# Splitting the last contraction's tokens into 384 and 128 instead of two halves of 256, with the second part's output products on VectorE alone

## The chip, the cores and the metric

The kernel runs on one core of a Trainium2 chip. The metric is the device time of one execution in microseconds, as the median of several runs. TensorE (PE) multiplies matrices into PSUM, VectorE (DVE), ScalarE (ACT) and GpSimd (POOL) work on elements, and SyncE (SP) issues the transfers between memory and the core's buffers.

## The reference, cut to what matters

Two layers on an input of 512 tokens with 1024 channels, all in float32. The whole ends like this:

```
h = h + (silu(gate) * val) @ w_down        # w_down: 2816 x 1024, layer 1
y = h * rsqrt(mean(h*h over channels) + 1e-6) * final_norm_g
```

Only these two lines bear on the change: the last down-projection's contribution to the residual h, and the final norm, whose mean runs over all 1024 channels of a token, so that no token's output can be formed before the last channel tile of that token is done.

## The kernel before

The residual h lies in SBUF with channels on the partitions: eight tiles (d = 0 to 7) of 128 channels by 512 tokens, together `hall`. A float32 product is made of three matmuls in rounded fp32 (fp32r): `mms` (lines 145 to 151) multiplies, for every block of 128 input channels, the weights' high part with the data's high part, the high with the low, and the low with the high. Each of these matmuls loads its own 128 x 128 weights.

The down-projection of layer 1 has 22 input blocks. They are done in chunks; the last chunk, blocks 18 to 21, is done by `last_down` (lines 842 to 863) in two parts of H = 256 tokens, so that the final norm of the first part can run beside the contraction of the second. A part t consists of eight channel tiles; `half` makes one tile with 4 x 3 = 12 matmuls, and `final_tile` (lines 867 to 881) then adds the result to h on VectorE (through the helper at line 418), squares it on ScalarE (line 876), sums the squares into `acc` on GpSimd (line 880; those of the last two tiles go to the statistics as separate inputs), and scales h by the norm's weight on ScalarE (line 881). The weights of all eight tiles are kept, and the eight tiles of part 1 follow those of part 0 in the order of the program.

`stats` (line 184) sums the squares over the channels with small fp32 matmuls (`sum_mm`, line 213: for each block of 128 tokens two matmuls of 64 columns, for each of three inputs). Every plain fp32 matmul shows as two instructions in the trace. `inv_rms_sqrt` (lines 216 to 226) makes the reciprocal root with a ScalarE square root, a VectorE reciprocal and a Newton step. `spreader` (line 236) then spreads it over the 128 partitions with one fp32 matmul per block of 128 tokens (line 241) into the PSUM tile `pbc`, and copies that to SBUF on ScalarE (`rs`, line 244), because GpSimd takes its factor from SBUF. `pst` and `pbc` share one PSUM buffer. `final_out` (lines 883 to 891) multiplies: four products of two tiles each (512 elements per partition), three on VectorE with `pbc` as factor, the fourth on GpSimd with `rs`; each product is stored by a transfer from SyncE's queue.

The program's order around the end is: the eight tiles of part 0; tile 0 of part 1; the statistics of part 0; tiles 1 to 3; the output of part 0; tiles 4 to 7; statistics and output of part 1. The framework's scheduler may shift single instructions within this.

Of the kernel before, what the change touches and what calls it, by code (L numbers as in the profile page):

```python
# [9 lines left out]
F32 = mybir.dt.float32  # L10
# [3 lines left out]
ALU = mybir.AluOpType  # L14
PSUM = bass.MemoryType.PSUM

P = 128
T = 512
KD = 8
NFF = 22  # L20
CH = (((0, 8), (8, 16), (16, 22)), ((0, 6), (6, 12), (12, 18)))
H = T // 2
EPS = 1e-6
LAG = (2, 3)
LATE = 2
# [28 lines left out]
def trunk(ctx: ExitStack, tc: tile.TileContext, x, pra, prb, eva, evu, evv, evo, evos, bmat, bmatz, cmat, wglu,  # L54
          wst, bs, odi, odo, up, dn, out):
    nc = tc.nc
    V, G, S, PE = nc.vector, nc.gpsimd, nc.scalar, nc.tensor

    cp = ctx.enter_context(tc.tile_pool(name="cp", bufs=1))
# [6 lines left out]
    def pt(name):  # L66
        return ps.tile([P, T], F32, tag="mm", name=name)

    def gt(name, dt=F32R):
        return gp.tile([P, T], dt, tag="g", name=name)  # L70
# [3 lines left out]
    hall = cp.tile([P, KD, T], F32, name="hall")  # L74
# [8 lines left out]
    warm = gt("warm", F32)  # L83
    V.memset(warm[:, :H], 1.0)
    pwarm = ps2.tile([P, T], F32, tag="aux", name="pwarm")
    for _ in range(NWARM):
        PE.matmul(pwarm[:, :H], lhsT=warm[:, :P], rhs=warm[:, :H], start=True, stop=True)
    onesd = cp.tile([P, 2], F32, name="onesd")
    V.memset(onesd, 1.0 / (KD * P))
    epsb = cp.tile([P, 1], F32, name="epsb")  # L90
    epsq = cp.tile([P, 1], F32, name="epsq")
    V.memset(epsb, EPS)
    S.activation(epsq, epsb, AF.Square)
# [51 lines left out]
    def mms(dst, hi, lo, xs, ks, first, last):  # L145
        for k in ks:
            xh, xl = xs[k]
            c = slice((k - first) * P, (k - first + 1) * P)
            PE.matmul(dst, lhsT=hi[:, c], rhs=xh, start=(k == first), stop=False)  # L149
            PE.matmul(dst, lhsT=hi[:, c], rhs=xl, start=False, stop=False)  # L150
            PE.matmul(dst, lhsT=lo[:, c], rhs=xh, start=False, stop=(k == last))  # L151
# [21 lines left out]
    def newton(m, y, n, tag):  # L173
        t = cp.tile([P, 8], F32, tag="nt", name=f"nt{tag}", bufs=2)[:, :n]
        ti = t.bitcast(I32)
        yi = y.bitcast(I32)
        V.tensor_scalar(out=ti, in0=m.bitcast(I32), scalar1=1, scalar2=None, op0=ALU.arith_shift_right)
        V.tensor_scalar(out=yi, in0=ti, scalar1=-1, scalar2=0x5F3759DF, op0=ALU.mult, op1=ALU.add)
        for _ in range(3):
            V.scalar_tensor_tensor(out=t, in0=y, scalar=-0.5, in1=y, op0=ALU.mult, op1=ALU.mult)  # L180
            V.tensor_tensor(out=t, in0=t, in1=m, op=ALU.mult)
            V.scalar_tensor_tensor(out=y, in0=t, scalar=1.5, in1=y, op0=ALU.add, op1=ALU.mult)

    def stats(tag, t0=0, n=4, extra=(), inv=None):


        parts = [acc[:, t0 * P:(t0 + n) * P]] + list(extra)
        pst = ps2.tile([P, T], F32, tag="aux", name=f"pst{tag}")
        for q, a in enumerate(parts):
            sum_mm(pst, a, n, q == 0, q == len(parts) - 1)  # L190
        return (inv or inv_rms)(pst, tag, n)

    def wide_stats(tag):
# [5 lines left out]
        def spread():  # L199
# [4 lines left out]
            V.scalar_tensor_tensor(out=t, in0=y, scalar=-0.5, in1=y, op0=ALU.mult, op1=ALU.mult)  # L204
            V.scalar_tensor_tensor(out=t, in0=pst, scalar=EPS, in1=t, op0=ALU.add, op1=ALU.mult)
            V.scalar_tensor_tensor(out=y, in0=t, scalar=1.5, in1=y, op0=ALU.add, op1=ALU.mult)
# [3 lines left out]
    def sum_mm(pst, a, n, first, last):  # L210
        for i in range(n):
            for e in (0, 64):
                PE.matmul(pst[e:e + 64, 2 * i:2 * i + 2], lhsT=a[:, i * P + e:i * P + e + 64], rhs=onesd,
                          start=first and i == 0, stop=last and i == n - 1)

    def inv_rms_sqrt(pst, tag, n):
# [3 lines left out]
        S.activation(s, src, AF.Sqrt, bias=epsb)  # L220
        V.tensor_scalar(out=m, in0=src, scalar1=EPS, scalar2=None, op0=ALU.add)
        V.reciprocal(y, s)
# [5 lines left out]
    def inv_rms(pst, tag, n):  # L228
        m = cp.tile([P, 8], F32, tag="m", name=f"m{tag}", bufs=2)[:, :n]
        y = cp.tile([P, 8], F32, tag="rt", name=f"rt{tag}", bufs=2)[:, :n]  # L230
        V.tensor_scalar(out=m, in0=pst[:, :2 * n].rearrange("p (i t) -> p i t", t=2)[:, :, 0],
                        scalar1=EPS, scalar2=None, op0=ALU.add)
        newton(m, y, n, tag)
        return y, spreader(y, tag, n)

    def spreader(y, tag, n):
        def spread():
            w = min(n, 4)
            pbc = ps2.tile([P, T], F32, tag="aux", name=f"pbc{tag}")
            for i in range(w):  # L240
                PE.matmul(pbc[:, i * P:(i + 1) * P], lhsT=y[:, i:i + 1].to_broadcast([P, P]), rhs=ident,
                          start=True, stop=True)
            rs = cp.tile([P, T], F32, tag="rs", name=f"rs{tag}")
            S.copy(rs[:, :w * P], pbc[:, :w * P])
            return rs, pbc
        return spread
# [29 lines left out]
    fsq = {}  # L276
# [78 lines left out]
    def v_norm():  # L355
        ss = sp.tile([P, 4], F32, name="ss")
        rv = sp.tile([P, 4], F32, name="rv")
        for t in range(4):
            q = sp.tile([P, 768], F32, tag="vsq", name=f"vsq{t}")
            S.activation(q, vg[t], AF.Square, accum_out=ss[:, t:t + 1])  # L360
        V.tensor_scalar(out=ss, in0=ss, scalar1=1.0 / 768.0, scalar2=EPS, op0=ALU.mult, op1=ALU.add)
        newton(ss, rv, 4, "v")
# [54 lines left out]
    def ttt(o, a, b, op):  # L417
        V.tensor_tensor(out=o, in0=a, in1=b, op=op)  # L418
# [422 lines left out]

    def last_down(gk, a, d):
        def half(t, e, hi, lo):
            p = pt(f"pl{t}_{e}")[:, :H]
            c = slice(t * H, (t + 1) * H)
            mms(p, hi, lo, {k: (gk[k][0][:, c], gk[k][1][:, c]) for k in range(a, NFF)},
                range(a, NFF), a, NFF - 1)
            final_tile(t, e, p)

        def f(hi, lo):  # L850
            kept.append((hi, lo))
            half(0, d, hi, lo)
            if d == 0:
                S.activation(epsq, acc[:, :1], AF.Sqrt)
            if d == KD - 1:
                for e in range(KD):
                    half(1, e, *kept[e])
                    if e == 0:
                        y0 = stats("fin0", 0, 2, fsq[0], inv_rms_sqrt)
                    if e == 3:  # L860
                        final_out(0, y0)
                final_out(1, stats("fin1", 2, 2, fsq[1], inv_rms_sqrt))
        return f

    kept = []

    def final_tile(t, d, p):
        c = slice(t * H, (t + 1) * H)
        ttt(h[d][:, c], h[d][:, c], p, ALU.add)
        if d == 0:  # L870
            S.activation(acc[:, c], h[d][:, c], AF.Square)
        else:
            late = d >= KD - 2
            sq = (gt(f"sqf{t}_{d}", F32) if late else
                  cp.tile([P, T], F32, tag="sq", name=f"sqf{t}_{d}", bufs=2))[:, :H]
            S.activation(sq, h[d][:, c], AF.Square)
            if late:
                fsq.setdefault(t, []).append(sq)
            else:
                G.tensor_tensor(out=acc[:, c], in0=acc[:, c], in1=sq, op=ALU.add)  # L880
        S.activation(h[d][:, c], h[d][:, c], AF.Copy, scale=pb[:, B_GFIN + d:B_GFIN + d + 1])

    def final_out(t, y):
        rs, pbc = y[1]()
        c = slice(t * H, (t + 1) * H)
        for q in range(4):
            o = gt(f"out{t}_{q}", F32).rearrange("p (d t) -> p d t", t=H)
            e, r = (G, rs) if q == 3 else (V, pbc)
            e.tensor_tensor(out=o, in0=hall[:, 2 * q:2 * q + 2, c],
                            in1=r[:, :H].unsqueeze(1).to_broadcast([P, 2, H]), op=ALU.mult)  # L890
            nc.sync.dma_start(out[t, :, 2 * q:2 * q + 2, :], o)

    def next_norm(col, tag, new):
        def f(d):
# [118 lines left out]
    w = gt("onesw", F32)[:, :P]  # L1013
# [87 lines left out]
```

## Time and profile before

| | us |
|---|---|
| median of 3 runs | 1064.66 |
| lowest and highest | 1063.97, 1065.13 |
| the profiled execution | 1063.25 |
| its span, first to last instruction | 1061.5 |
| mean granted TensorE clock | 0.998 of full speed |

The profile comes from one execution, whose own time is 1.4 us under the median. Times in the trace's rows are microseconds from the start of the span; a row of the timeline gives start, duration, engine, line, operation, output and inputs, shapes and the count of instructions merged into it. Matmuls are pipelined: the recorded duration of one is longer than the distance to the next one's start, so that a price of a matmul in a stream is read from starts.

### The profile page before, as it was taken

Reading aid. Unit: us, or ns where it says so; the run is one execution under the profiler, and the core shown is the slowest. Engines: PE = TensorE matmul, PEld = TensorE weight load, DVE = VectorE, ACT = ScalarE, POOL = GpSimd, SP = SyncE. Lnnn points to the kernel's source line nnn. Section 1 sums busy time; section 2 is a strip of 40 time slices with the busy share of each in tenths; the row PEclk is TensorE's granted clock in tenths of the full one; section 3 lists DMA queues with packets and bytes.
Section 4 is the critical chain, followed back from the end, with each engine's and each line's share of the span. In section 5 each row is a group of like instructions: output and inputs, shape, how many; then the busy total and the mean of one; then the engine's idle time right before and its main releaser. Section 6 shows DMA issues by size and latency. Waiting matters only on the chain.

```text
span 1061.5 us, 12932 instructions
## 1 busy us (share of the span) xinstructions
PE 1049.3 (99%) x5098; PEld 875.9 (83%) x5098; DVE 669.5 (63%) x926; ACT 421.3 (40%) x567; POOL 134.4 (13%) x120
## 2 busy tenths in 40 slices
PE   9999999999999999999999999999999999999997
PEld 7978788888888888888888888888888888888886
DVE  7996679866356653566576564678645664666543
ACT  5563355443133431344423222444423432444344
POOL 3010031110001000012211110302100100011002
PEclk9999999999999999999999999999999999999999
DMA  7362332333332332223322321423233223222222
GB/s 261 123 130 81 99 100 99 101 98 99 100 99 99 96 90 96 97 80 89 130 93 86 99 99 60 139 84 102 73 120 99 90 81 128 98 93 79 88 80 80
DMA packets 40125, 107.21 MB, mean 101 GB/s; under 512 B 10368, under 2 KB 11392, under 8 KB 40064
## 3 DMA queue, kind: packets, MB, share of 16 engines
q1 hardware_dynamic: 39920, 106.12, 32.0%
q8 instruction: 40, 0.66, 0.3%
q10 hardware_dynamic: 144, 0.26, 0.1%
q14 instruction: 21, 0.17, 0.0%
HBM read 103.08 MB, written 3.28 MB: 100 GB/s over the span
## 4 chain that ended last, share of the span: by engine, by line
PE 97%; ACT 1%; DMA 1%; DVE 0%; SPq 0%; issue 0%; POOL 0%; DVEq 0%; ACTq 0%; POOLq 0%
PE pf L151 15%; PE pf L150 15%; PE pf L149 15%; PE pd L151 11%; PE pd L150 11%; PE pd L149 11%; PE po L151 1%; PE po L149 1%; PE po L150 1%; PE pe L149 1%; PE pe L150 1%; PE pe L151 1%; PE pv L314 1%; PE pv L315 1%; PE pv L313 1%; PE phu L149 1%
## 5 line engine op out<-in xcount | busy, mean ns | idle before, releaser
L125 ACT CAST whi<-raw 128x1024 fp32r<-128x1024 f32 (+2 forms) x203 | 198.4, 980 | 450.5 <-PE pd L150 200.7
L151 PE MATMUL pf<-xhf,wlo 128*128 128x512 f32 x704 | 273.9, 389 | 0.0
L150 PE MATMUL pf<-xlf,whi 128*128 128x512 f32 x704 | 273.6, 389 | 0.0
L149 PE MATMUL pf<-xhf,whi 128*128 128x512 f32 x704 | 273.5, 389 | 0.0
L126 DVE TENSOR_TENSOR wlo<-raw,whi 128x1024 fp32r<-128x1024 f32 (+3 forms) x204 | 246.5, 1209 | 39.9 <-ACT whi L125 39.6
L150 PEld LDWEIGHTS pf<-xlf,whi 128*128 128x128 f32 x704 | 132.2, 188 | 27.8 <-DVE xlf L159 0.2
L149 PEld LDWEIGHTS pf<-xhf,whi 128*128 128x128 f32 x704 | 132.2, 188 | 27.5
L151 PEld LDWEIGHTS pf<-xhf,wlo 128*128 128x128 f32 x704 | 132.2, 188 | 27.2
L418 DVE TENSOR_TENSOR hs<-pf,rsf 128x512 f32<-128x512 f32 x88 | 60.5, 691 | 126.4 <-PE pf L151 126.3
L815 POOL TENSOR_TENSOR cv<-cv,cv 128x512 f32<-128x512 f32 x44 | 58.5, 1329 | 571.6 <-DVE cv L788 529.3
L418 DVE TENSOR_TENSOR hall<-hall,pd 128x512 f32<-128x512 f32 x48 | 32.9, 686 | 101.1 <-PE pd L151 101.1
L151 PE MATMUL pd<-xhm,wlo 128*128 128x512 f32 x192 | 74.7, 389 | 0.0
L150 PE MATMUL pd<-xlm,whi 128*128 128x512 f32 x192 | 74.7, 389 | 0.0
L149 PE MATMUL pd<-xhm,whi 128*128 128x512 f32 x192 | 74.7, 389 | 0.0
L786 ACT ACTIVATE cv<-hs,pb 128x512 f32<-128x512 f32 x88 | 71.3, 815 | 7.4 <-DVE hs L418 6.0
L788 DVE SCALAR_TENSOR_TENSOR cv<-hs,pb,cv 128x512 f32<-128x512 f32 x88 | 66.1, 751 | 2.7
L787 DVE SCALAR_TENSOR_TENSOR cv<-hs,pb,cv 128x512 f32<-128x512 f32 x88 | 67.5, 769 | 0.0
L812 ACT ACTIVATE cv<-cv 128x512 f32<-128x512 f32 x44 | 27.8, 632 | 81.5 <-DVE cv L788 81.4
L149 PEld LDWEIGHTS pd<-xhm,whi 128*128 128x128 f32 x192 | 36.0, 188 | 7.6
L150 PEld LDWEIGHTS pd<-xlm,whi 128*128 128x128 f32 x192 | 36.0, 188 | 7.5
L151 PEld LDWEIGHTS pd<-xhm,wlo 128*128 128x128 f32 x192 | 36.0, 188 | 7.4
L171 POOL TENSOR_TENSOR acc<-acc,sqf 128x512 f32<-128x512 f32 x14 | 23.1, 1653 | 56.4 <-ACT sqf L170 56.1
(587 smaller groups left out, 1569.7 us busy)
## 6 DMA issues: line engine op xcount, KB each, us to landing
raw<-up SPq DMA_DIRECT2D x88, 512.0 KB, 3.4
raw<-dn SPq DMA_DIRECT2D x32, 384.0 KB, 3.2
raw<-odi SPq DMA_DIRECT2D x24, 512.0 KB, 3.4
raw<-dn SPq DMA_DIRECT2D x16, 512.0 KB, 3.5
raw<-odo SPq DMA_DIRECT2D x8, 512.0 KB, 3.4
raw<-evo SPq DMA_DIRECT2D x8, 384.0 KB, 3.2
raw<-eva SPq DMA_DIRECT2D x7, 384.0 KB, 6.6
raw<-evu SPq DMA_DIRECT2D x5, 512.0 KB, 4.5
```

The lines of the kernel that those rows point to most:

```text
L125: S.copy(hi[:, c], r[:, c])
L126: V.tensor_tensor(out=lo[:, c], in0=r[:, c], in1=hi[:, c].bitcast(F32), op=ALU.subtract)
L149: PE.matmul(dst, lhsT=hi[:, c], rhs=xh, start=(k == first), stop=False)
L150: PE.matmul(dst, lhsT=hi[:, c], rhs=xl, start=False, stop=False)
L151: PE.matmul(dst, lhsT=lo[:, c], rhs=xh, start=False, stop=(k == last))
L171: eng.tensor_tensor(out=acc, in0=acc, in1=sq, op=ALU.add)
L418: V.tensor_tensor(out=o, in0=a, in1=b, op=op)
L786: S.activation(o, src[:, 2:T + 2], AF.Identity, scale=w2, bias=b)
L787: V.scalar_tensor_tensor(out=o, in0=src[:, 1:T + 1], scalar=w1, in1=o, op0=ALU.mult, op1=ALU.add)
L788: V.scalar_tensor_tensor(out=o, in0=src[:, 0:T], scalar=w0, in1=o, op0=ALU.mult, op1=ALU.add)
L812: S.activation(c, c, AF.Silu)
L815: G.tensor_tensor(out=c, in0=c, in1=fp["gate"], op=ALU.mult)
```

## The change

The token parts become 0 to 384 and 384 to 512 (`TP`). The statistics of the first part cover three blocks of 128 tokens, those of the second one block. The output of part 0 is made in eight products of one tile (384 elements), of which GpSimd takes three and VectorE five; the output of part 1 in four products of two tiles (256 elements), all on VectorE from PSUM, and the copy of the factor to SBUF is left out there. The output tensor is laid out accordingly, and the host puts the parts together.

```
+TP = ((0, 384), (384, 512))
...
     def spreader(y, tag, n):
-        def spread():
+        def spread(copy=True):
...
+            if not copy:
+                return None, pbc
             rs = cp.tile([P, T], F32, tag="rs", name=f"rs{tag}")
             S.copy(rs[:, :w * P], pbc[:, :w * P])
             return rs, pbc
...
         def half(t, e, hi, lo):
-            p = pt(f"pl{t}_{e}")[:, :H]
-            c = slice(t * H, (t + 1) * H)
+            c = slice(*TP[t])
+            p = pt(f"pl{t}_{e}")[:, :c.stop - c.start]
...
-                        y0 = stats("fin0", 0, 2, fsq[0], inv_rms_sqrt)
+                        y0 = stats("fin0", 0, 3, fsq[0], inv_rms_sqrt)
                     if e == 3:
                         final_out(0, y0)
-                final_out(1, stats("fin1", 2, 2, fsq[1], inv_rms_sqrt))
+                final_out(1, stats("fin1", 3, 1, fsq[1], inv_rms_sqrt))
...
     def final_tile(t, d, p):
-        c = slice(t * H, (t + 1) * H)
+        c = slice(*TP[t])
...
     def final_out(t, y):
-        rs, pbc = y[1]()
-        c = slice(t * H, (t + 1) * H)
-        for q in range(4):
-            o = gt(f"out{t}_{q}", F32).rearrange("p (d t) -> p d t", t=H)
-            e, r = (G, rs) if q == 3 else (V, pbc)
-            e.tensor_tensor(out=o, in0=hall[:, 2 * q:2 * q + 2, c],
-                            in1=r[:, :H].unsqueeze(1).to_broadcast([P, 2, H]), op=ALU.mult)
-            nc.sync.dma_start(out[t, :, 2 * q:2 * q + 2, :], o)
+        rs, pbc = y[1](copy=t == 0)
+        c = slice(*TP[t])
+        w = c.stop - c.start
+        n = t + 1
+        for q in range(KD // n):
+            dd = slice(n * q, n * q + n)
+            o = gt(f"out{t}_{q}", F32)[:, :n * w].rearrange("p (d t) -> p d t", t=w)
+            e, r = (G, rs) if t == 0 and q in (2, 5, 7) else (V, pbc)
+            e.tensor_tensor(out=o, in0=hall[:, dd, c],
+                            in1=r[:, :w].unsqueeze(1).to_broadcast([P, n, w]), op=ALU.mult)
+            a = KD * c.start + n * w * q
+            nc.sync.dma_start(out[:, a:a + n * w].rearrange("p (d t) -> p d t", t=w), o)
```

## Rows read from the trace of the kernel before

**Rows 1.** The page: TensorE's busy time, share of the span and instructions (with the other engines'), the granted clock in 40 slices of the span, and the engines' shares of the chain that ended last.

```profile
PE 1049.3 (99%) x5098; PEld 875.9 (83%) x5098; DVE 669.5 (63%) x926; ACT 421.3 (40%) x567; POOL 134.4 (13%) x120
...
PEclk9999999999999999999999999999999999999999
...
PE 97%; ACT 1%; DMA 1%; DVE 0%; SPq 0%; issue 0%; POOL 0%; DVEq 0%; ACTq 0%; POOLq 0%
```

**Rows 2.** The chain of waits at the end, in order of time: start and length in us, engine, output, line.

```profile
1051.83 0.13 PE pl L151
...
1051.99 0.43 DVE hall L418
...
1052.44 0.42 ACT sqf L876
...
1052.89 0.51 ACT hall L881
1053.40 0.23 ACT srfin L220
...
1054.62 0.70 PE pbcfin L241 x4
...
1055.39 0.38 ACT rsfin L244
...
1055.80 0.69 DVE out L889
```

**Rows 3.** Timeline of TensorE: first and last start of 9 matmul distances at 384 columns (the first projection), and of 24 at 256 columns (the second part of the last contraction).

```profile
41.51 0.33 PE L313 MATMUL pv<-whi,xhm 128*128 128x384 f32 x1
...
43.07 0.33 PE L313 MATMUL pv<-whi,xhm 128*128 128x384 f32 x1
...
1047.47 0.28 PE L149 MATMUL pl<-g_18h,whi 128*128 128x256 f32 x1
...
1050.35 0.28 PE L149 MATMUL pl<-g_18h,whi 128*128 128x256 f32 x1
```

**Rows 4.** Groups by line and form, weight loads (PEld): count, busy us, mean ns of one, idle before.

```profile
L149 PEld LDWEIGHTS pl<-g_18h,whi 128*128 128x128 f32 x16 | 3.1, 191 | 0.1
...
L213 PEld LDWEIGHTS pstfin<-onesd,sqf 128*64 128x64 f32 x32 | 1.3, 137 | 0.6 <-ACT sqf L876 0.5
```

**Rows 5.** Timeline: two weight loads that follow the gating step's short matmuls, and 18 of those matmuls (plain fp32, 128 columns, two instructions for each product).

```profile
84.61 0.19 PEld L149 LDWEIGHTS phu<-xhm,whi 128*128 128x128 f32 x1
84.73 0.19 PEld L150 LDWEIGHTS phu<-xlm,whi 128*128 128x128 f32 x1
...
104.31 2.27 PE L396 MATMUL pg<-wt,vg 128*128 128x128 f32 x18
```

**Rows 6.** Timeline of TensorE: statistics matmuls of part 0 (8 for one input), the spread of part 0, and the spread of part 1. One recorded matmul lasts 0.20 us in the first kind and 0.275 in the others.

```profile
1040.11 0.40 PE L213 MATMUL pstfin<-onesd,acc 128*64 128x2 f32 x8
...
1045.96 0.60 PE L241 MATMUL pbcfin<-ident,rtfin 128*128 128x128 f32 x4
...
1054.62 0.68 PE L241 MATMUL pbcfin<-ident,rtfin 128*128 128x128 f32 x4 [1.31 <-DVE rtfin L225]
```

**Rows 7.** Groups by line and form of VectorE, ScalarE and GpSimd: count, busy us, mean ns of one, idle before. The adds at 256 and 512 columns, squares at 256 and 512, scales at 256 and 512, GpSimd's sums at 256 and products at 512.

```profile
L418 DVE TENSOR_TENSOR hall<-hall,pl 128x256 f32<-128x256 f32 x16 | 6.6, 420 | 13.0 <-PE pl L151 13.0
L418 DVE TENSOR_TENSOR hall<-hall,pd 128x512 f32<-128x512 f32 x48 | 32.9, 686 | 101.1 <-PE pd L151 101.1
...
L876 ACT ACTIVATE sqf<-hall 128x256 f32<-128x256 f32 x14 | 5.7, 415 | 6.8 <-DVE hall L418 5.4 <-DVE ntfin L224 1.3
L170 ACT ACTIVATE sqf<-hall 128x512 f32<-128x512 f32 x14 | 8.6, 618 | 0.0
L881 ACT ACTIVATE hall<-hall,pb 128x256 f32<-128x256 f32 x16 | 8.0, 507 | 0.4
L158 ACT ACTIVATE xhf<-hall,pb 128x512 fp32r<-128x512 f32 x16 | 11.5, 720 | 5.2 <-DVE hall L418 5.2
...
L880 POOL TENSOR_TENSOR acc<-acc,sqf 128x256 f32<-128x256 f32 x10 | 7.4, 739 | 43.5 <-ACT sqf L876 43.5
L889 POOL TENSOR_TENSOR out<-hall,rsfin 128x512 f32<-128x512 f32 x2 | 2.6, 1286 | 4.4 <-ACT rsfin L244 4.4
```

**Rows 8.** Timeline of VectorE: the three products of part 0, and the two adds that had waited behind them.

```profile
1047.03 1.88 DVE L889 TENSOR_TENSOR out<-hall,pbcfin 128x512 f32<-128x512 f32 x3 [0.81 <-ACT rsfin L244]
1048.83 0.74 DVE L418 TENSOR_TENSOR hall<-hall,pl 128x256 f32<-128x256 f32 x2
```

**Rows 9.** Timeline of SyncE's queue: the issues of part 1's output. The third and fourth are merged in one row, which ends 0.91 us after the third's start; a row of the fourth alone stands below it.

```profile
1056.51 0.33 SPq L891 DMA_DIRECT2D out<-out  x1
...
1057.11 0.33 SPq L891 DMA_DIRECT2D out<-out  x1
...
1057.54 0.91 SPq L891 DMA_DIRECT2D out<-out  x2
...
1058.04 0.41 SPq L891 DMA_DIRECT2D out<-out  x1
```

**Rows 10.** The transfers of part 1's output, GB/s in 40 slices of 0.15 us from 1056 to 1062 us; and the time from issue to landing of the eight output transfers.

```profile
GB/s 0 0 0 0 0 0 0 0 41 314 382 396 410 342 382 396 410 341 383 396 410 341 383 396 396 341 410 123 0 0 0 0 0 0 0 0 0 0 0 0
...
DMA to landing us min/median/max: 2.1/2.3/3.1
```

**Rows 11.** The waits between 1050 and 1062 us: who waited for whom, us in total, times, longest.

```profile
DVE out L889 <- ACT rsfin L244: 1.3, 1, 1.3
```

More of the change, by code (lines that the diff above doesn't have):

```diff
@@ L874, in final_tile @@
             sq = (gt(f"sqf{t}_{d}", F32) if late else
-                  cp.tile([P, T], F32, tag="sq", name=f"sqf{t}_{d}", bufs=2))[:, :H]
+                  cp.tile([P, T], F32, tag="sq", name=f"sqf{t}_{d}", bufs=2))[:, :c.stop - c.start]
             S.activation(sq, h[d][:, c], AF.Square)
@@ L1094 @@
             for n in _INS]
-    args.append(nc.dram_tensor("out", (2, P, KD, T // 2), F32, kind="ExternalOutput").ap())
+    args.append(nc.dram_tensor("out", (P, KD * T), F32, kind="ExternalOutput").ap())
     with _tile.TileContext(nc, schedule_with_timeline_sim=True) as tc:
@@ L1099 @@
     got = r.results[0]["out"]
-    return _np.ascontiguousarray(got.transpose(0, 3, 2, 1)).reshape(1, T, KD * P)
+    parts = [got[:, KD * a:KD * b].reshape(P, KD, b - a).transpose(2, 1, 0) for a, b in TP]
+    return _np.ascontiguousarray(_np.concatenate(parts, axis=0)).reshape(1, T, KD * P)
```

## Prediction

> **What bounds the kernel now.** I read the page first: TensorE is busy 99% of the span, 97% of the chain that ended last is TensorE, and the granted clock is full (2.4 GHz, a digit 9) in all forty slices [rows 1]. So a microsecond added to TensorE's stream is a microsecond of the kernel. Then the end of the chain of waits [rows 2]: after the last contraction matmul (1051.83 + 0.13 = 1051.96) TensorE only serves a serial tail: add, square, scale, square root, small VectorE steps, spread matmuls, a ScalarE copy, products, transfers, until 1061.5. That is 9.54 us during which the kernel is bound by latencies. The change trades between these two stretches: it adds to the stream and cuts the tail. The other views give prices: starts of matmuls by width [rows 3], weight loads [rows 4, 5], the statistics matmuls [rows 6], durations by shape [rows 7], VectorE and SyncE in order [rows 8, 9], the transfers [rows 10] and the waits [rows 11].
>
> **The change, part by part.** The sum is made against the profiled execution, 1063.25 us; the median of the runs is 1064.66, so I add the difference to the median. About 2.1 us (0.2%) is what a measurement of this kernel can tell from no change.
>
> *First part, 384 columns.* 8 tiles x 12 matmuls = 96. At 256 columns, 24 matmuls lie between two starts 2.88 us apart: 0.1200 us each; at 384 columns, 9 take 1.56 us: 0.1733 [rows 3]. 96 x 0.0533 = **+5.1 us**, all on TensorE.
>
> *Second part, 128 columns.* Again 96 matmuls, each with its own 128-column weight load. The trace has no rounded-fp32 (fp32r) matmul of 128 columns, so I bound it. The line through the two widths falls 0.000417 us per column and leaves 0.0133 at zero columns; at 128 columns it gives 0.067 us: lower end. Above, the nearest row of that width is the plain fp32 matmul of the gating step: two instructions for each product, 18 instructions in 2.27 us, less one's 0.275 of depth over 17 steps = 0.117 each [rows 5], so 0.235 a product; without the small loss per instruction the two take 2 x 0.108 (the spread matmuls: (0.60 - 0.275)/3 [rows 6]) = 0.216: upper end. Between them the weight load decides. A load of 64 columns is recorded with 137 ns and one of 128 with 191 [rows 4]: 54 ns for 64 columns, so 0.108 us of a 128-column load is throughput and only the rest is pipeline depth. With the 0.0133 that every fp32r matmul here pays, that is **0.121 us**, whatever the stream is. The two loads at 84.61 and 84.73, behind the gating step's short matmuls, stand 0.12 apart [rows 5], and that is the row nearest to the case: a load that waits for nothing but the load before it. Then the second part costs 96 x (0.121 - 0.120) = **+0.1 us**: the shorter matmuls save nothing. By 0.067 the term would be -5.1 us, by 0.216 it would be +9.2.
>
> A rule that gives another price: the Trainium skill, "TensorE: Matmul & The Clock Gate", section "Back-to-back issue gap", has about 81 ns for each matmul in a stream of load and matmul pairs of 128 columns. With it, as an estimate, the term would be -3.7 us and the whole change about -0.7 us; no run here has shown such a stream in fp32r, and the lengths of the loads [rows 4] speak against it.
>
> *Statistics of the first part.* Three column blocks instead of two: each of three inputs takes 12 matmul instructions instead of 8, so 12 more at (0.40 - 0.20)/7 = 0.029 us [rows 6] = +0.35 us; its spread takes 6 instead of 4 at 0.108 [rows 6] = +0.22. Together **+0.6 us** on TensorE.
>
> *First output.* Eight products of one tile (384 elements) instead of four of 512, five on VectorE, three on GpSimd, and eight transfers instead of four. Not on the end's path as long as the second part lasts: from its fourth tile to its end are 4 x 12 x 0.121 = 5.8 us. VectorE needs five products of about 0.55 us (between 0.42 for 256 and 0.69 for 512 [rows 7]), some 2.5 us, and its adds wait meanwhile, as they did before (three products, 1.88 us, then two adds together [rows 8]). GpSimd does three at about 1.0 us (between its 0.74 for 256 and 1.29 for 512 [rows 7]), ahead of the sums of squares of tiles 4 and 5; all of that ends over a microsecond before the last tile. SyncE issues eight at about 0.43 us [rows 9], 3.4 us, with nothing queued behind but the last output. If that cover is gone (second part short), it costs up to 1.7 us; see the first rival. In the first part a tile takes 2.08 us of TensorE, more than its add (0.55), its square and scale (0.52 + 0.61) or its GpSimd sum (1.0): hidden.
>
> *Tail.* Per step, from [rows 2, 7]: the add 0.42 to 0.29 (slope (0.686 - 0.420)/256 per column): -0.13. The square 0.415 to 0.31: -0.10. The scale, which stands ahead of the square root on ScalarE, 0.51 to 0.40: -0.11. The square root and the four small VectorE steps: unchanged, they are all overhead. The spread, two instructions instead of four: (0.68 - 0.275)/3 = 0.135 each [rows 6]: -0.27. The copy: VectorE's products wait today for ScalarE's copy of the same PSUM tile [rows 11], 1055.32 to 1055.80; without it they follow TensorE directly: -0.46. The products: three of 512 on VectorE last 1.88 us [rows 8]; four of 256 take 0.42 + 3 x 0.32 (two adds of that size took 0.74 [rows 8]) = 1.38: -0.50. GpSimd's product (1.29) ran beside them and isn't missed. So the last product ends 1.57 us sooner. Transfers: before, 1.05 MB kept the DMA engines full from about 1057.2 to 1060.2 [rows 10], 2.16 us beyond the last issue at 1058.04 [rows 9]. Now 0.52 MB comes in pieces of 128 KB that need about 0.36 us each at the same rate, less than the 0.43 between issues, so nothing piles up: 0.75 us from issue to data plus 0.36 = 1.1 us beyond the last issue: -1.05. If a transfer instead needs its shortest recorded 2.1 us to land [rows 10], nothing is gained there. Tail: **-2.6 us**, bounds -1.6 and -2.8.
>
> *Sum.* 5.1 + 0.1 + 0.6 - 2.6 = **+3.2 us**: 1066.4 in the profiled execution, 1067.8 against the median, 0.3% slower. With 0.108 to 0.130 for the short matmul (-1.2 to +0.9) and the tail's bounds: +1.7 to +5.1.
>
> **Rivals.**
> *The short matmul streams at its width (not slower).* If a 128-column load hides behind 0.067 us, the two parts cost TensorE what two of 256 did: 96 x (0.1733 + 0.0667 - 0.2400) = 0, and 0.6 - 2.6 = -2.0 us remain: 1062.7. But then tiles come every 0.80 us, and after the fourth only 3.2 us are left: VectorE's five products and four adds need about 3.6 us, and ScalarE's squares and scales (0.71 a tile) can only follow; up to 1.7 us of the gain goes into that, so 1062.7 to 1064.4. For: the line through two widths is straight to 256. Against: the load rows. It decides from a price of 0.109 on: below that the change is no longer slower by more than 0.2%. The Trainium skill's "TensorE: Matmul & The Clock Gate", section "Wait — 56ns, not 53.3ns?", has the width over 2.4 GHz plus about 2.5 ns between matmuls back to back, which is this rival's rule; the rows here agree in the slope and show 13 ns, not 2.5, beside it [rows 3].
> *A short fp32r matmul falls back to the price of plain fp32.* 96 x (0.216 - 0.121) = +9.1 more: +12.3, 1077.0. For: 256 is the narrowest fp32r operand anywhere in this trace, so nothing shows that the single pass holds below. Against: from 384 to 256 columns the price falls with the width, with no sign of a step to come.
> *The copy's removal removes no wait* (the products then wait as long for something else): 0.46 of the gain is gone, 1068.3; inside the forecast's range.
>
> **How the numbers follow.** Load-bound at about 0.12: 0.60. Streaming: 0.22. Plain fp32's price: 0.15. Anything else, a scheduler that orders the end otherwise for instance: 0.03. The prediction is the first case, 1067.8; its own range is 1066.4 to 1069.8. The range given reaches down to the streaming case, 1062.7, and up to 1070.0; it leaves out the plain-fp32 case and small tails. Slower by over 0.2% (above 1066.8): 0.60 x 0.78 + 0.15 + 0.01 = 0.63. Faster (below 1062.5): 0.22 x 0.4 + 0.01 = 0.10. Within: 0.27.
>
> **What the profile after would show.** Starts 0.173 apart in the first part; in the second 0.12 apart if I am right, 0.067 or 0.22 if a rival is, with the weight loads at the same distance. The last contraction matmul some 5.8 us later than before; from it to the end of the span some 6.9 us instead of 9.5; the products starting within 0.05 us of the spread's end with no ScalarE copy between; four issues about 0.43 apart and no backlog of transfers. I am wrong if short matmuls start much under 0.11 apart, or if the tail stays above 8 us.

## The result, and the profile after

The changed kernel took 1067.31 us (median of 19 runs), the kernel before, in runs beside it, 1064.14 (19 runs): 3.2 us or 0.3% slower. The ratio of all the runs is 1.0050, with a 95% interval of 1.0033 to 1.0066. It is larger than that of the medians because the runs of the changed kernel are spread in a way that those of before are not: twelve lie between 1065.4 and 1067.8, seven between 1072.6 and 1077.6. The kernel before stays between 1062.6 and 1066.3. The profiled execution is one of the seven: 1072.95 us, span 1071.2.

First the page of the changed kernel: TensorE's row, and the granted clock in 40 slices.

```profile
span 1071.2 us, 12944 instructions
...
PE 1060.6 (99%) x5098; PEld 887.4 (83%) x5098; DVE 669.7 (63%) x929; ACT 421.2 (39%) x566; POOL 135.4 (13%) x121
...
PEclk9999999999999999999999999999999999999995
```

TensorE's busy time has grown by 11.3 us with the same number of matmuls [rows 1], and the last slice of the clock shows a 5. The view by stretches says where: the wide part, the narrow part in two pieces, and the rest. After the stretch come its length, busy us (and instructions) of PE, PEld, DVE, ACT, POOL, then the granted clock, DMA share and GB/s.

```profile
1026.70:1043.40 16.70, 16.70 (x98) 16.70 (x97) 4.56 (x8) 9.37 (x16) 5.07 (x5) 1.00 0.00 1
1043.40:1048.70 5.30, 5.30 (x72) 5.12 (x71) 1.77 (x8) 2.57 (x7) 0.21 (x1) 1.00 0.00 0
1048.70:1063.20 14.50, 14.50 (x71) 14.38 (x70) 3.76 (x10) 3.87 (x12) 4.98 (x8) 0.50 0.31 110
1063.20:1071.20 8.00, 1.72 (x15) 1.29 (x14) 2.40 (x10) 0.97 (x3) 0.00 (x0) 0.50 0.20 66
```

From about 1048.7 us on TensorE runs at 1.2 GHz instead of 2.4, in the middle of the second part's narrow matmuls and without having been idle: it is busy for 5.30 of the 5.30 us ahead of the fall. The timeline of TensorE shows the matmuls on both sides of it:

```profile
1048.19 0.27 PE L150 MATMUL pl<-g_20h,whi 128*128 128x128 f32 x1
1048.30 0.28 PE L151 MATMUL pl<-g_20l,whi 128*128 128x128 f32 x1
1048.41 0.28 PE L152 MATMUL pl<-g_20h,wlo 128*128 128x128 f32 x1
1048.52 0.28 PE L150 MATMUL pl<-g_21h,whi 128*128 128x128 f32 x1
...
1048.97 0.41 PE L150 MATMUL pl<-g_18h,whi 128*128 128x128 f32 x1
1049.18 0.41 PE L151 MATMUL pl<-g_18l,whi 128*128 128x128 f32 x1
1049.39 0.41 PE L152 MATMUL pl<-g_18h,wlo 128*128 128x128 f32 x1
1049.61 0.41 PE L150 MATMUL pl<-g_19h,whi 128*128 128x128 f32 x1
```

Three narrow matmuls take 0.33 us before the fall and 0.64 after it: 0.111 and 0.213 each, against 0.120 for the 256-column ones of before [rows 3]. Some sixty of them at the lower clock cost 60 x 0.102 = 6.1 us; the spread's six matmuls (1.59 us instead of 0.88 in e8 below) and the tail (7.96 instead of 7.49) make up most of the rest of the 7.5 us by which this execution lies above the fastest ones (1065.4). With all 96 at half clock it would be 9.8 us plus the same rest, an estimate that comes to the runs at 1077; none of these was profiled.

The same kernel profiled a second time (e8 below) did not fall until the end. Its stretches, in the same columns, are those that answer to the prediction's sum:

```profile
1028.50:1045.30 16.80, 16.80 (x99) 16.76 (x98) 4.57 (x8) 9.37 (x16) 5.07 (x5) 1.00 0.00 1
1045.30:1058.30 13.00, 13.00 (x141) 12.75 (x141) 5.44 (x18) 6.31 (x18) 5.21 (x8) 1.00 0.19 65
1058.30:1061.10 2.80, 1.07 (x14) 0.73 (x14) 1.00 (x7) 0.92 (x3) 0.00 (x0) 1.00 0.75 267
```

The first of its wide and the first of its narrow matmuls, 96 wide ones apart (16.67 us, 0.1736 each):

```profile
1028.59 0.33 PE L150 MATMUL pl<-g_18h,whi 128*128 128x384 f32 x1
...
1045.26 0.22 PE L150 MATMUL pl<-g_18h,whi 128*128 128x128 f32 x1
```

And the end of its chain of waits, which answers to [rows 2]:

```profile
1058.18 0.13 PE pl L152
...
1058.33 0.30 DVE hall L421
...
1058.65 0.32 ACT sqf L879
...
1059.00 0.40 ACT hall L884
1059.40 0.22 ACT srfin L221
...
1060.29 0.17 DVE rtfin L226
...
1060.60 0.47 PE pbcfin L242 x2
...
1061.09 0.42 DVE out L895
```

In that execution the last contraction lasts from its first matmul at 1028.59 to 1058.31, 29.72 us; before it was 1027.07 to 1051.96, 24.89. That is +4.83. From there to the end of the span (1065.8) are 7.49 us instead of 9.54: -2.05. Together +2.8 us, with a full clock. The kernels here also differ from execution to execution by steps of some 2 us, because the clock is at half for a moment around 65 us in some (granted 1.00, 0.89 or 0.77 between 55 and 70 us). That fall is of another kind: TensorE had been idle ahead of it (in e8 it was busy for 0.10 of the 1.00 us from 64 to 65). Hence spans are compared from the first matmul of the last contraction, and medians over all runs.

### The profile page after: what moved, and what is told of

It reads as the page before. It is cut to its first block, busy times and chain, and to the rows that moved or that the text cites. A ratio compares the mean times of both kernels' runs of the same rounds, so it can differ in the third digit from the quotient of the medians.

```text
span 1071.2 us, 12944 instructions
## 1 busy us (share of the span) xinstructions
PE 1060.6 (99%) x5098; PEld 887.4 (83%) x5098; DVE 669.7 (63%) x929; ACT 421.2 (39%) x566; POOL 135.4 (13%) x121
## 4 chain that ended last, share of the span: by engine, by line
PE 98%; ACT 1%; DMA 0%; DVE 0%; issue 0%; SPq 0%; POOL 0%; DVEq 0%; POOLq 0%
PE pf L151 15%; PE pf L150 15%; PE pf L152 15%; PE pd L150 11%; PE pd L151 11%; PE pd L152 11%; PE po L152 1%; PE po L150 1%; PE po L151 1%; PE pe L150 1%; PE pl L150 1%; PE pl L152 1%; PE pl L151 1%; PE pv L317 1%; PE pe L151 1%; PE pe L152 1%
```

## The experiments

Each run's number of executions and range is given with its median; "before" beside them had medians of 1064.5 to 1064.7 throughout (27 to 29 runs in each batch).

**e1_equal_nocopy**: the tail's part of the change alone, on the kernel before.

```
-        rs, pbc = y[1]()
+        rs, pbc = y[1](copy=t == 0)
...
-            e, r = (G, rs) if q == 3 else (V, pbc)
+            e, r = (G, rs) if t == 0 and q == 3 else (V, pbc)
```

> The kernel before (two parts of 256) with one part of the change alone: in the second part's output the factor isn't copied to SBUF and all four products (512 elements) are on VectorE from PSUM. Theory 1 (the products waited for the copy): they start 0.46 us sooner behind the spread, four of them last 2.5 us instead of 1.9, the transfers start 0.46 sooner and stay the bound: 0.5 us faster than before, within a measurement's error. Theory 2 (another wait takes the copy's place): no change to 0.2 us slower. Under both, every contraction matmul starts 0.120 us after the one before, and the clock is full in all runs up to the last contraction matmul.

Measured: 1063.97 us (12 runs, 1062.32 to 1065.88), ratio to before 0.9993 (0.9983 to 1.0003); a second time, as **e11_equal_nocopy_again**, 1063.89 (11 runs, 1062.31 to 1065.58), 0.9996 (0.9986 to 1.0007).

> e1_equal_nocopy again, beside e9 and e10: 0.4 to 0.6 us faster than the kernel before in like runs, as in its first measurement, 1064.0.

The chain of waits of e1 has the first product directly behind the spread:

```profile
1055.96 0.70 PE pbcfin L241 x4
...
1056.68 0.69 DVE out L891
```

0.02 us instead of 0.48 [rows 2]: the wait for the copy is gone and none took its place. From the last contraction matmul (1053.30) to the end (1062.4) it is 9.1 us instead of 9.54, so 0.44 of the expected 0.46 arrives. Theory 1 holds in the profile; in the times the gain is 0.6 us of medians twice, which the intervals don't separate from nothing.

**e2_split_only**: the split with the copy and GpSimd's product back.

```
-        rs, pbc = y[1](copy=t == 0)
+        rs, pbc = y[1]()
...
-            e, r = (G, rs) if t == 0 and q in (2, 5, 7) else (V, pbc)
+            e, r = (G, rs) if q in ((2, 5, 7) if t == 0 else (3,)) else (V, pbc)
```

> The changed kernel with the split into 384 and 128 alone: in the second part's output the copy is back, and the fourth product is on GpSimd as before. Expected: the contraction as in the changed kernel, 0.173 us a matmul in the first part, 0.111 or 0.213 in the second, with the clock falling at a moment that differs from run to run; the tail 0.3 to 0.5 us longer than the changed kernel's. If the clock's fall belonged to the part without the copy, this one would show none: the runs would then all lie within 2 us of each other.

Measured: 1067.86 us (10 runs), seven between 1065.7 and 1067.9, three between 1076.7 and 1077.7; ratio 1.0057 (1.0029 to 1.0086). So the runs about 10 us above the others, which are the falls, come with the split and not with the missing copy. Its profiled execution had none until 1058 us; from the last contraction matmul (1056.10) to the end (1064.0) are 7.9 us, 0.4 more than in the changed kernel, as expected.

**e3_wide256** and **e4_wide192**: the second part's matmuls take 256, or 192, columns, of which the last 128 are used.

```
-            p = pt(f"pl{t}_{e}")[:, :c.stop - c.start]
+            w = 256 if t else c.stop - c.start
+            c = slice(c.stop - w, c.stop)
+            p = pt(f"pl{t}_{e}")[:, :w]
...
-            final_tile(t, e, p)
+            final_tile(t, e, p[:, w - (TP[t][1] - TP[t][0]):])
```

> The changed kernel, but the second part's 96 matmuls take 256 columns (tokens 256 to 511) and only the last 128 of the result are used: twice the columns for the same weight loads, everything else alike. Theory 1 (the clock falls because the second part's matmuls are narrow: TensorE streams only 128 columns for each 128-column load): starts 0.120 apart, full clock in every run up to the last contraction matmul, and 96 x 0.009 = 0.9 us over the changed kernel's undisturbed runs (1065.4): 1066.3, all runs within 1.5 us of each other, none above 1070. Theory 2 (it falls because of the waits at the statistics and the output, or of where the part stands): runs up to 1078 as in the changed kernel.

> As e3_wide256 with 192 columns. Theory 1 (a 128-column weight load sets the distance of short matmuls): starts 0.111 us apart at full clock, the same as at 128 columns. Theory 2 (the distance follows the columns below some width too): 0.0133 + 192 x 0.000417 = 0.093. For the clock: if narrowness decides, falls are rarer or later than at 128 columns; with none of them the time is 1065.4 by theory 1 and 1063.7 by theory 2.

Measured: e3 1068.59 us (5 runs, 1068.34 to 1069.33), ratio 1.0036 (1.0023 to 1.0050); e4 1067.10 (12 runs, 1065.32 to 1069.17), ratio 1.0023 (1.0013 to 1.0033). No run of either lies above 1070. The second part of e3, and that of e4, by stretches:

```profile
1045.40:1059.30 13.90, 13.90 (x141) 13.47 (x139) 5.53 (x18) 6.40 (x18) 5.25 (x8) 1.00 0.18 63
```

```profile
1044.70:1057.90 13.20, 13.20 (x144) 12.87 (x142) 5.53 (x18) 6.33 (x18) 5.23 (x8) 1.00 0.23 79
```

Full clock in both. In e4 three of the 192-column matmuls take 0.33 us:

```profile
1049.33 0.27 PE L150 MATMUL pl<-g_19h,whi 128*128 128x192 f32 x1
...
1049.66 0.27 PE L150 MATMUL pl<-g_20h,whi 128*128 128x192 f32 x1
```

From the first narrow matmul to the end of the last the second part lasts 13.05 us with 128 columns (e8), 13.13 with 192 and 13.95 with 256: between 128 and 192 the columns cost nothing, and the starts are 0.111 apart in both. Twice the columns for 0.9 us and the clock stays up. So what sets the distance at 128 and 192 columns isn't the columns. As for the falls, no run of these 17 shows one, against 14 of 41 with 128 columns for each load (the changed kernel, e8 and e2); chance alone would give that in well under one of a hundred cases. The statistics and the output stand at the same place in all of them. e3's median is 2.3 us over the 1066.3 that I gave, in which the 0.9 us of this stretch stood already. Of the 2.3, 2.0 is the moment around 65 us, which I hadn't allowed for: the profiled execution has it, and its last contraction starts at 1028.71 instead of 1026.69 in the changed kernel's profile without it. The other four have the like mean clock (0.995 or 0.996).

**e5_halfload**: in blocks 19 to 21 of the second part 64 weight columns are loaded instead of 128, at the same 128 token columns; this leaves their share of the contraction out of the result.

```
+                p2 = pt(f"pm{e}")[:64, :c.stop - c.start]
+                for k in range(a, NFF):
+                    q, m, f = (p, P, a) if k == a else (p2, 64, a + 1)
...
+                    PE.matmul(q, lhsT=hi[:, o:o + m], rhs=xh, start=(k == f), stop=False)
```

> The changed kernel, but in the second part the matmuls of blocks 19 to 21 load 64 of the 128 output channels (64 weight columns instead of 128; the 128 token columns are streamed as before), and their results go to a PSUM tile that nobody reads: the last contraction is left out for these blocks. Theory 1 (the load of 128 weight columns sets the 0.111 us between narrow matmuls): 0.111 for block 18, and 0.067 (128 columns on the line of the wider ones) for the others; 72 x 0.044 = 3.2 us less than the changed kernel in like runs. Theory 2 (any fp32r matmul of 128 columns takes 0.111, whatever it loads): 0.111 throughout and no change. For the clock: with 128 columns each 0.067 us the array streams most of the time again, and I expect no fall before the end; if it is the width as such that counts, falls as before.

Timeline of its TensorE, second part: `pl` is block 18 with the whole load, `pm` the others with half of it.

```profile
1045.43 0.27 PE L859 MATMUL pl<-g_18l,whi 128*128 128x128 f32 x1
1045.54 0.27 PE L860 MATMUL pl<-g_18h,wlo 128*128 128x128 f32 x1
1045.66 0.23 PE L858 MATMUL pm<-g_19h,whi 128*64 128x128 f32 x1
1045.72 0.22 PE L859 MATMUL pm<-g_19l,whi 128*64 128x128 f32 x1
1045.78 0.22 PE L860 MATMUL pm<-g_19h,wlo 128*64 128x128 f32 x1
```

0.111 with the whole load, 0.060 with half of it, the stream alike: the weight load sets the distance, theory 1. All ten runs lie between 1063.55 and 1065.41 (median 1064.95); in the profiled one the clock is full all through the last contraction. That contraction is 3.7 us shorter than in e8 (26.02 instead of 29.72), somewhat more than expected, since I had put 0.067 for the half load. In the medians 2.6 us of it arrive (against e8's, which has falls in it), because the shorter second part no longer covers the first output: the last statistics waited 1.4 us for VectorE's five products, and the tail lasts 9.0 us instead of 7.5.

**e6_interleave**: four narrow tiles moved between the wide ones.

```
             half(0, d, hi, lo)
+            if 2 <= d <= 5:
+                half(1, d - 2, *kept[d - 2])
...
-                for e in range(KD):
+                for e in range(4, KD):
```

> The changed kernel with the narrow tiles 0 to 3 done between the wide tiles 2 to 6 of the first part, so that 4 narrow tiles in a row are left at the end (5.3 us of narrow matmuls instead of 10.7); the first part's statistics follow the fifth narrow tile, its output the sixth. The same matmuls in another order. If the fall of the clock needs a long run of narrow matmuls: no run 9 us above the others any more, at most 5.3 us are lost and in fewer runs; the rest of the runs as the changed kernel's (1065.4 to 1067.8) plus up to 1.5 us for the first output, which is now nearer to the end. If any narrow stretch can bring it: a third of the runs above 1070 again.

Measured: 1072.70 us (4 runs, 1071.35 to 1073.41), ratio 1.0075 (1.0059 to 1.0091). The profiled run fell, and the mean clocks of all four (0.990 to 0.992) say that all did. The stretches: interleaved tiles, the narrow run up to the fall, the rest of it, the tail.

```profile
1032.50:1048.30 15.80, 15.80 (x109) 15.80 (x109) 3.92 (x9) 8.48 (x19) 6.12 (x8) 1.00 0.00 1
1048.30:1052.20 3.90, 3.90 (x59) 3.73 (x59) 1.19 (x5) 2.02 (x5) 0.46 (x1) 1.00 0.00 0
1052.20:1059.20 7.00, 7.00 (x34) 6.82 (x33) 0.88 (x5) 0.99 (x3) 0.45 (x1) 0.51 0.01 2
```

My expectation fell: four narrow tiles in a row are enough, and here the fall came in every run. Narrow tiles of 1.3 us between wide ones kept the full clock in the profiled run. The timeline of TensorE at the tail, with the idle time ahead of the instruction and its releaser in brackets, shows a second loss:

```profile
1062.00 0.35 PE L214 MATMUL pstfin<-onesd,acc 128*64 128x2 f32 x3 [2.79 <-DVE out L897]
```

With the first output so near the end, the last statistics waited 2.79 us for VectorE's products, which read the PSUM buffer that the statistics use next.

**e7_pair**: in the second part the data's high and low parts lie in one tile, and one load of the high weights serves both.

```
+                PE.matmul(p.rearrange("p (s t) -> p s t", s=2), lhsT=hi[:, o], rhs=g2s[k][:, :, c],
+                          start=(k == a), stop=False)
+                PE.matmul(p[:, :w], lhsT=lo[:, o], rhs=gk[k][0][:, c], start=False, stop=(k == NFF - 1))
+            ttt(h[e][:, c], h[e][:, c], p[:, w:], ALU.add)
```

> The changed kernel with two of the three loads of each block merged in the second part: the data's high and low parts lie side by side in one tile, one matmul with the high weights streams both (256 columns into two halves of the PSUM tile), one with the low weights streams 128; VectorE adds both halves, one add more per tile. If loads set the price: 32 x (0.120 + 0.111) = 7.4 us instead of 96 x 0.111 = 10.7 for the second part, 3.3 us less than the changed kernel in like runs, less 0.3 for the additional add on the tail, and no fall of the clock: about 1064.2, within 0.1% of the kernel before, all runs below 1067. If the price is one of columns: 384 columns a block in either way, no gain, 0.3 us slower.

Measured: 1066.69 us (12 runs, 1064.64 to 1068.26), ratio 1.0019 (1.0009 to 1.0029). No run above 1070. Timeline of its TensorE, two blocks:

```profile
1046.15 0.33 PE L865 MATMUL pl<-gp,whi 128*128 128x256 f32 x1
1046.32 0.22 PE L867 MATMUL pl<-gp,wlo 128*128 128x128 f32 x1
1046.38 0.33 PE L865 MATMUL pl<-gp,whi 128*128 128x256 f32 x1
1046.55 0.22 PE L867 MATMUL pl<-gp,wlo 128*128 128x128 f32 x1
1046.60 0.33 PE L865 MATMUL pl<-gp,whi 128*128 128x256 f32 x1
```

A block takes 0.23 us instead of 0.333 for the same 384 columns: the price is one of loads, as expected, and the second part gains 3.3 us (9.73 from its first matmul to the end of the last, instead of 13.04). But VectorE, in order, did this:

```profile
1055.02 2.41 DVE L914 TENSOR_TENSOR out<-hall,pbcfin 128x384 f32<-128x384 f32 x5
1057.34 0.80 DVE L421 TENSOR_TENSOR hall<-hall,pl 128x128 f32<-128x128 f32 x3
```

The contraction ends at 1055.69, and the last adds wait for the first output's products until 1057.34; the tail is 10.1 us instead of 7.5, with one add more in it. Most of the gain was turned into this wait: against e8's median, which has falls in it, 0.8 us are left.

**e9_pair_early**: e7 with the first output behind the second narrow tile.

```
-                    if e == 3:
+                    if e == 1:
                         final_out(0, y0)
```

> e7_pair with the first part's output two tiles earlier (behind the second narrow tile instead of the fourth). In e7_pair the last two adds waited 1.9 us for the five products of the first output, and the tail lasted 10.3 us from the last contraction matmul instead of 7.5. If that wait is the whole of it, the products now end before the last contraction matmul, the tail is about 7.8 us, and the time 2.3 us below e7_pair's: 1064.4, as the kernel before or a little faster. If it is not (the additional adds and the copy of the factor keep VectorE and ScalarE late anyway), it stays at 1066 to 1067.

Measured: 1066.58 us (11 runs, 1065.19 to 1068.94), ratio 1.0025 (1.0015 to 1.0034). Its spread still comes 7.5 us after the first narrow matmul (1051.27 after 1043.81), and the products run from 1052.87, as late as in e7 (7.5 and 9.1 us): the framework's scheduler had put them at the same place in both. The edit changed nothing (the tail is 10.2 us), so whether an earlier output brings the rest of the gain wasn't tried by it and stays open.

**e10_equal_pair**: e1 with the paired matmul in the first part, by the same lines as e7.

> e1_equal_nocopy (two parts of 256, no copy) with the paired matmul in the first part, where its additional add is hidden: 512 columns with one load of the high weights, 256 with the low ones. 32 x (0.2267 + 0.1200 - 3 x 0.1200) = -0.4 us on TensorE: 0.9 us faster than the kernel before in like runs, 1063.6. If the additional add of 0.42 us a tile isn't hidden, or the pair costs TensorE as much as the two matmuls, it is as e1_equal_nocopy.

Measured: 1064.50 us (11 runs, 1061.87 to 1065.34), ratio 0.9995 (0.9986 to 1.0005). In the profile a pair takes 0.35 us for three times 0.12, as worked out, and the last contraction is 24.48 us instead of e11's 24.88. The 0.9 us that I expected in the median did not come: it lies at that of the kernel before (1064.47) and 0.6 us above e11's, and the intervals don't tell the three apart.

**e8_after_again**: the changed kernel unaltered.

> The changed kernel again, beside the others on the same chip. Expected: 1065.4 to 1067.8 in about two of three runs, 1072 to 1078 in the others, those with a mean granted clock of 0.990 or less; in a run of the first kind narrow matmuls 0.111 apart all through the second part and 7.5 us from the last of them to the end.

Measured: 1067.52 us (12 runs), eight between 1065.6 and 1068.2, four between 1073.7 and 1076.8; ratio 1.0051 (1.0026 to 1.0076). As expected, tail included (7.49 us). With the first 19 runs, 11 of 31 fell early enough to lie above 1070.

## Why the prediction was right, and where it was not

The forecast was 1067.8, 0.3% slower, within 1062.7 to 1070.0; the median is 1067.31. The mechanism is the one forecast: the wide matmuls pay for their columns, the narrow ones don't save theirs because each loads 128 weight columns. e5 shows it (half the load, half the distance), e4 (more columns, same distance) and e7 (fewer loads, less time for the same columns) too. The streaming rival is refuted by all three, the plain-fp32 rival by the narrow matmul's 0.111 us, and the rival that the copy's removal removes no wait by e1.

That the number came out within 0.5 us is partly luck. Without the seven falls, which I had not foreseen, the median of the changed kernel is 1066.85, 2.7 us above the kernel before and not 3.2; and the 2.7 hides two errors of my sum that go against each other.

*First part.* 0.1736 us a matmul in e8, as taken from [rows 3]. Right.

*Second part.* I put 0.121 us, a load of 0.108 [rows 4] plus the 0.0133 that the wider matmuls pay. It is 0.111: at 128 and 192 columns the 0.0133 doesn't come on top of the load. 96 x 0.010 = 1.0 us too much. The Trainium skill, "TensorE: Matmul & The Clock Gate", section "LDWEIGHTS (loading the stationary operand)", has columns over 1.2 GHz for a load, which is 107 ns for 128. The trace's 111 ns between starts agree with that at the full clock; at the lower clock it has 213. The 81 ns of the same page's section "Back-to-back issue gap", which the prediction weighed, are not what these fp32r matmuls take.

*Statistics.* In the profiles the contraction grew by 4.83 us at full clock; the matmuls' +5.1 and -0.9 leave 0.6 for the statistics. Right.

*Tail.* -2.05 instead of -2.6 us. Up to the start of the products it is 2.78 us instead of 3.84: -1.06, against -1.07 forecast, every step within 0.04 of what was worked out. The products last 1.42 instead of 1.88: -0.46 against -0.50. The term that failed is the transfers: -1.05 forecast. In e8 the last issue stands at 1062.94,

```profile
1062.94 0.40 SPq L898 DMA_DIRECT2D out<-out  x1
```

and the span ends 2.86 us later; before it was 3.46 [rows 9]. That is -0.6 with everything behind the last issue in it. The pieces of 128 KB didn't come at the 370 GB/s of the larger ones [rows 10]: e8's GB/s in slices of 0.15 us from 1060 us,

```profile
GB/s 348 369 82 10 0 0 0 0 0 0 0 0 0 0 0 48 280 341 198 239 355 260 185 348 301 130 348 335 130 0 0 0 0 0 0 0 0 0 0 0
```

show 0.52 MB over 2.0 us from 1062.3 on, in four bursts: 340 to 355 GB/s at their height, 130 to 200 between them, about 260 on average. There was no backlog, as forecast, but the last piece, behind which nothing comes, has its data from 1063.8 to 1064.3, 0.5 us instead of the 0.36 worked out, and they begin 0.9 us after its issue instead of 0.75. So the data end 1.4 us beyond the last issue, where 1.1 was forecast. Whether the pieces' size or something else makes them slower no run here shows.

The two errors (1.0 us too slow in the second part, 0.55 too fast in the tail) partly cancel: the sum corrected for both is +2.8, e8's two stretches give +2.8, and the medians without falls +2.7.

*What the prediction missed.* That the clock can fall. I priced the narrow matmul at the clock of the trace before, where no stretch with TensorE busy was at half, and none of my rivals had a lower one. Nor is the clock full in all forty slices, as I read the row of digits: from 1057 us on, with TensorE idle, the granted clock of before is 0.50, and the last slice still shows a 9 (it means 90% or more). The falls cost 6 to 11 us against the median of the other runs, in 11 of 31 runs, all of them outside the range. In the median of the first 19 runs they count for 0.5 us; in their mean, 5.5 us above that of the kernel before, for 3.2, some three fifths of the loss. In the first output my cover was right for the changed kernel, and where the second part got shorter (e5, e7), its loss was near the 1.7 us that I had put as the most: the last statistics waited 1.4 and 1.9 us for VectorE's products, which read the PSUM buffer that they use next.

What stays open is why the fall comes in some runs and not in others at the same instructions, and at a moment that differs. No run here shows it.

## What to carry to other kernels

A matmul whose columns would stream in less time than its weight load takes costs the load, not its columns: here, with 128 weight columns in fp32r, up to about 235 columns, an estimate from the 0.111 us of the load and the line through the wider matmuls ((0.111 - 0.0133) / 0.000417). Splitting a contraction unevenly below that lengthens the wide part and hardly shortens the narrow one. To make a narrow part cheap, let one load serve more columns, and check what the shorter part used to cover. And look at the granted clock of every run after a change to the shapes of the matmuls: a busy TensorE in the profile is no assurance that the clock stays up.

The copy's removal (e1, e11) is the part of the change that gains without a price elsewhere: 0.44 us in the profile, 0.6 in the medians, below what these runs separate from nothing. No version here beats the kernel before clearly.

## What the runs showed of the hardware

- The clock fell with TensorE busy without a gap in two profiles (the changed kernel and e6), each time within a run of matmuls of 128 columns with one load of 128 weight columns each. By the times and mean clocks it did so in 11 of 31 runs of the changed kernel, 3 of 10 of e2 and 4 of 4 of e6. In no profile did it fall during the last contraction where a load serves more columns or is shorter, and no run is above 1070: e3 (5 runs), e4 (12), e5 (10), e7 (12) and e9 (11).
- At the lower clock the distance of load-bound matmuls nearly doubles too, from 0.111 to 0.213 us: the weight load slows with TensorE's granted clock.
- fp32r matmuls of 256, 384 and 512 columns that load 128 weight columns each pay some 13 ns beside their columns; with 64 weight columns (e5) 128 columns took 0.060 us, 7 ns over the 53 of their columns (128 x 0.000417).
